# Six split-weight tiles of a two-layer hybrid block: homes of their own at six addresses modulo 128 bytes, instead of three rotating buffers each

## The chip, the cores and the metric

One core of a Trainium2 chip runs the whole program in one launch. The metric is the device time in microseconds of one execution; the median of three runs stands for a kernel.

## The reference, cut to what matters

Two layers, each a mixer and a feed-forward part, on 256 tokens of width 1024, all in float32:

```python
def reference(x, ...):
    for l in range(DEPTH):                       # DEPTH = 2
        h = rms_norm(x, norm_mix_w[l])
        x = x + hybrid_mixer(h, w_in[l], ...)    # attention with a top-64 index, and an SSD scan
        h = rms_norm(x, norm_ffn_w[l])
        x = x + conv_glu_ffn(h, ffn_w_up[l], ...)
    return rms_norm(x, norm_final_w)

def conv_glu_ffn(h, w_up, conv_w, conv_b, w_down):
    u = causal_dwconv(h @ w_up, conv_w, conv_b)
    gate, val = u[..., :FFN_DIM], u[..., FFN_DIM:]
    return (jax.nn.silu(gate) * val) @ w_down
```

Nearly all arithmetic is in products of a 256-token activation with a weight matrix: the wide input projection of the mixer (9,320 columns), three output projections, and the up and down projections of the feed-forward part.

## The kernel before, in words

Activations lie transposed: features on the 128 partitions, the 256 tokens along the free dimension. A float32 product is made of three products in the faster type float32r: both operands are split into a high part (a cast to float32r) and a low part (what the cast left), and high x high, high x low and low x high are summed in PSUM.

The weights come as chunks of at most 128 x 1024 float32, that is 4096 bytes a partition. The list `order` says in which order the chunks are loaded and split. For each chunk, `load_some` issues one DMA into a `raw` buffer (five of them, `RAW_BUFS`), ScalarE casts raw to the high tile `whi` (L199), and VectorE subtracts and writes the low tile `wlo` (L200). `take` does this as far ahead as buffers allow: three pairs (`SPLIT_BUFS`), so the cast for a chunk waits until the products with the chunk three before it are done. Some chunks, those in `early`, are split into activation tiles that happen to be free (names that begin with e: `es`, `ez`, `ex`, `eths`, `ehxh`, `ehxl`, `ebig`, `eXt`, `epT`); they don't use the pairs.

`feed_high` (L370 and L371) multiplies `whi` with the high and the low activation, 16 matmuls a chunk; `feed_low` (L376) multiplies `wlo` with the high activation, 8 a chunk. Here the weight tile is the stationary operand, 128 columns loaded anew for every matmul, and the activation is the moving one, 256 columns. Only in the first five groups of a layer (L549 to L551) is it the other way round: the activation is loaded, and `whi` or `wlo` moves, 308 or 512 columns wide. `n_outer` takes one chunk for one output tile of 128 features, `k_outer` runs four output tiles side by side. Side work (index, attention and scan steps) is put between the products by three lanes of generators, and the order of each engine's instructions is fixed when the program is built.

The moving activations are `hxh`/`hxl` (normed input), `aH`/`aL` (attention out), `bH`/`bL` (SSD out), `mH`/`mL` (merged) and `fH`/`fL` (gated feed-forward), each in tiles of the pool `act`; the tags `s0` to `s3`, `z0` to `z3`, `x0` to `x3` of that pool are reused from stage to stage.

**Addresses.** A pool's tiles stand one behind the other, in the order of their first use, each size rounded up to 32 bytes; so offsets follow from the sizes. Modulo 128 bytes, the raw tiles, all three `whi` and all three `wlo` stand at 64 (the first `whi` at byte 44,608 of a partition). Of the moving tiles, `hxh`, `hxl`, `mH`, `mL`, and all of the tags s, z and x stand at 0, `big0` and `big1` (in which `bL` lies) and the `uh`, `ul` tiles of the first five groups at 64. Below "distance" means how far, modulo 128 bytes, the start of a stationary tile is from that of the moving tile (0 to 64).

Of the kernel before, what the change touches and what calls it, by code (L numbers as in the profile page):

```python
# [10 lines left out]
F32R = mybir.dt.float32r  # L11
# [7 lines left out]
P = 128  # L19
# [14 lines left out]
RAW_BUFS = 5  # L34
SPLIT_BUFS = 3

FIRST_PAIRS = 4


# [23 lines left out]
def hybrid_kernel(ctx: ExitStack, tc: tile.TileContext, a: dict, out: bass.AP):  # L63
# [1 line left out]

    const = ctx.enter_context(tc.tile_pool(name="const", bufs=1))
    wraw = ctx.enter_context(tc.tile_pool(name="wraw", bufs=RAW_BUFS))
    wsp = ctx.enter_context(tc.tile_pool(name="wsp", bufs=SPLIT_BUFS))
    act = ctx.enter_context(tc.tile_pool(name="act", bufs=1))
    tmp = ctx.enter_context(tc.tile_pool(name="tmp", bufs=2))  # L70
    psum = ctx.enter_context(tc.tile_pool(name="psum", bufs=2, space=PSUM))
# [25 lines left out]
    for l in range(L):  # L97
# [11 lines left out]
        for n in range(8):  # L109
            if n == FIRST_PAIRS:  # L110
                for i in range(16):
# [25 lines left out]
        make_early(base, EARLY_MIX)  # L137
        make_early(base + 20, EARLY_CONV)

    st = {"cur": 0, "prep": 0, "dma": 0, "now": 0, "mm": None}  # L140
    lanes = {"norm": [], "attn": [], "scan": []}

    def side(lane, gen, delay):
# [34 lines left out]
    def split_tiles(j):  # L178
        if j in early:
            t0, t1 = early[j]  # L180
            if t0 == t1:
                t = act.tile([P, 2, 8 * 128], F32R, name=f"e{t0}", tag=t0)
                return [t[:, 0], t[:, 1]]
            return [(tmp if t in ("Xt", "pT") else act).tile([P, 8 * 128], F32R, name=f"e{t}", tag=t, bufs=1)
                    for t in (t0, t1)]
        return [wsp.tile([P, 8 * 128], F32R, name=t, tag=t) for t in ("whi", "wlo")]

    def take():
        i = st["cur"]
        with tc.high_priority():  # L190
            load_some()
            while st["prep"] < len(order):
                j = order[st["prep"]]
                if j not in early and sum(k not in early for k in splits) == SPLIT_BUFS:
                    break
                src, b, c = chunks[j]
                hi, lo = (t[:, :b * c] for t in split_tiles(j))
                r = raws.pop(j)
                nc.scalar.copy(out=hi, in_=r)  # L199
                nc.vector.tensor_sub(lo, r, hi.bitcast(F32))  # L200
                splits[j] = [t.rearrange("p (b c) -> p b c", b=b) for t in (hi, lo)]
                st["prep"] += 1
                load_some()
        st["cur"] += 1
        if st["mm"] is not None:
            side_steps()
        return splits.pop(i)
# [197 lines left out]
    for l in range(L):  # L405
# [133 lines left out]
        for c in range(5):  # L539
            n = 308 if c < 2 else 512  # L540
            pss = [pst("acc", [P, n], 4) for _ in range(2)]
            for j in range(4):
                wh, wl = take()
                for kk in range(2):
                    k = 2 * j + kk
                    f, e = k == 0, k == KD - 1
# [5 lines left out]
            for t in range(2):  # L552
                r = nrm.cols[:, t:t + 1]
# [206 lines left out]
        def gate_and_project(n):  # L760
            finish("attn")
            th = gate(tmp.tile([P, T], F32, name="gv", tag="cv", bufs=3))
            ps = n_outer([(lambda k: aH[k // 4][:, k % 4, :], lambda k: aL[k // 4][:, k % 4, :], range(8))])
            nc.vector.scalar_tensor_tensor(mg[n], th, 1.0, ps, op0=OP.add, op1=OP.mult)

        for n in range(FIRST_PAIRS):
            gate_and_project(n)
# [38 lines left out]

        for n in range(FIRST_PAIRS, 8):
            gate_and_project(n)
# [89 lines left out]
    for c in range(2):  # L898
        for h in range(2):
# [4 lines left out]
            r = nrm.cols[:, c:c + 1]  # L904
# [89 lines left out]
```

## Time and profile before

| | us |
|---|---|
| median of 3 runs (lowest to highest) | 1089.46 (1084.34 to 1089.93) |
| profiled execution, its own time | 1091.08 |
| span of that execution | 1089.1 |
| TensorE busy with matmuls (share of the span) | 1064.4 (98%) |
| VectorE busy | 877.9 (81%) |
| ScalarE busy | 696.2 (64%) |
| GpSimd busy | 66.5 (6%) |
| granted TensorE clock, mean | 0.997 |

The span is the time from the first to the last instruction; the profiled execution's own time is 2.0 us longer. A matmul is shown as busy for some 0.28 us, though the next one starts after less than half of that: matmuls overlap, so it is the distance from one start to the next that says how fast they go, and the busy share alone doesn't.

### The profile page before, as it was taken

To read this page: it belongs to the slowest core of one execution; us is meant where nothing else is said; L and a number is where in the kernel's file an instruction comes from. 1 tells how busy PE (TensorE), PEld (TensorE's weight loads), DVE (VectorE), ACT (ScalarE), POOL (GpSimd) and SP (SyncE) were. 2 spreads that over 40 slices of the span, in tenths; PEclk is the share of its full clock that TensorE was granted. 3 is DMA by queue.
4 is the path that set the end of the run, shared out by engine and by line. 5 is a ranking of instruction groups with operands and counts; after the bars stand their busy time and mean duration, and the time that the engine had idled before them with its cause. 6 is when DMAs were issued, how large, how long until landed. Compare 5 with 4: busy or idle time off the path is not lost.

```text
span 1089.1 us, 22471 instructions
## 1 busy us (share of the span) xinstructions
PE 1064.4 (98%) x8704; PEld 1026.2 (94%) x8704; DVE 877.9 (81%) x1755; ACT 696.2 (64%) x1285; POOL 66.5 (6%) x74
## 2 busy tenths in 40 slices
PE   6999999999999999998999999999999999999997
PEld 5789989999999999998997999999999999999997
DVE  6898988879877899885668999887887878888643
ACT  5658878647555576665555699865665556666552
POOL 3000000022000200000100000000310020000010
PEclk9999999999999999999999999999999999999999
DMA  7546444555677346666645654555567761666661
GB/s 266 183 148 213 151 147 156 161 169 175 194 233 251 117 122 195 194 199 211 183 134 176 224 155 139 164 172 155 175 190 216 246 216 45 182 187 191 180 182 48
DMA packets 52841, 191.82 MB, mean 176 GB/s; under 512 B 5952, under 2 KB 6240, under 8 KB 51712
## 3 DMA queue, kind: packets, MB, share of 16 engines
q1 hardware_dynamic: 50832, 180.31, 53.8%
q0 software_dynamic: 1472, 9.17, 2.3%
q8 instruction: 68, 1.11, 0.4%
q10 hardware_dynamic: 432, 0.92, 0.2%
q14 instruction: 37, 0.30, 0.1%
HBM read 189.26 MB, written 1.11 MB: 175 GB/s over the span
## 4 chain that ended last, share of the span: by engine, by line
PE 85%; DMA 5%; ACT 4%; DVE 3%; issue 2%; DVEq 0%; ACTq 0%; POOLq 0%
PE acc L370 23%; PE acc L371 23%; PE acc L376 23%; PE acc L550 3%; PE acc L551 2%; PE acc L549 2%; DMA bc<-prd 2%; DMA raw<-in_wu_dram 2%; PE sb L705 1%; DVE wlo L200 1%; ACT whi L199 1%; PE sa L461 1%; DVE ul L327 1%; PE sa L589 1%; PE sa L614 1%
## 5 line engine op out<-in xcount | busy, mean ns | idle before, releaser
L199 ACT CAST whi<-raw 128x1024 fp32r<-128x1024 f32 (+2 forms) x320 | 331.9, 1040 | 225.1 <-PE acc L371 168.7
L200 DVE TENSOR_TENSOR wlo<-raw,whi 128x1024 fp32r<-128x1024 f32 (+2 forms) x320 | 387.0, 1212 | 107.5 <-ACT whi L199 103.1
L370 PE MATMUL acc<-hxh,whi 128*128 128x256 f32 x1456 | 353.3, 282 | 1.0 <-ACT ths L657 0.9
L371 PE MATMUL acc<-hxl,whi 128*128 128x256 f32 x1456 | 351.2, 281 | 0.0
L370 PEld LDWEIGHTS acc<-hxh,whi 128*128 128x128 f32 x1456 | 274.6, 189 | 2.7 <-issue 1.1
L371 PEld LDWEIGHTS acc<-hxl,whi 128*128 128x128 f32 x1456 | 274.7, 189 | 2.2 <-issue 1.9
L376 PE MATMUL acc<-hxh,wlo 128*128 128x256 f32 x1456 | 202.2, 280 | 0.0
L376 PEld LDWEIGHTS acc<-hxh,wlo 128*128 128x128 f32 x1456 | 183.0, 189 | 0.7 <-issue 0.7
L370 PE MATMUL acc<-fH,whi 128*128 128x256 f32 x352 | 84.6, 280 | 2.8 <-DVE xT L833 2.8
L371 PE MATMUL acc<-fL,whi 128*128 128x256 f32 x352 | 84.4, 280 | 0.0
L649 DVE SCALAR_TENSOR_TENSOR cv<-acc,half,cv 128x255 f32<-128x255 f32 (+2 forms) x144 | 67.1, 474 | 3.9 <-ACT cv L647 3.4
L370 PEld LDWEIGHTS acc<-fH,whi 128*128 128x128 f32 x352 | 66.6, 190 | 3.1 <-issue 3.0
L851 DVE SCALAR_TENSOR_TENSOR cv<-acc,small,cv 128x255 f32<-128x255 f32 (+1 forms) x144 | 68.4, 477 | 1.3
L371 PEld LDWEIGHTS acc<-fL,whi 128*128 128x128 f32 x352 | 66.6, 189 | 0.0
L370 PE MATMUL acc<-bH,whi 128*128 128x256 f32 x256 | 62.4, 280 | 0.1
L371 PE MATMUL acc<-bL,whi 128*128 128x256 f32 x256 | 62.3, 282 | 0.0
L337 POOL TENSOR_TENSOR ssq<-ssq,sq 128x256 f32<-128x256 f32 x30 | 27.1, 904 | 516.8 <-ACT sq L333 516.2
L549 PE MATMUL acc<-whi,uh 128*128 128x512 f32 (+1 forms) x112 | 42.0, 392 | 9.2 <-ACT whi L199 9.2
L376 PE MATMUL acc<-fH,wlo 128*128 128x256 f32 x352 | 50.1, 281 | 0.0
L370 PEld LDWEIGHTS acc<-bH,whi 128*128 128x128 f32 x256 | 48.1, 188 | 0.4 <-issue 0.4
L371 PEld LDWEIGHTS acc<-bL,whi 128*128 128x128 f32 x256 | 48.2, 188 | 0.0
L695 ACT ACTIVATE bc<-bc,nP 128x128 f32<-128x128 f32 x128 | 39.9, 390 | 11.6 <-DMA bc<-prd 11.5
(281 smaller groups left out, 1873.0 us busy)
## 6 DMA issues: line engine op xcount, KB each, us to landing
raw<-in_wu_dram SPq DMA_DIRECT2D x88, 512.0 KB, 3.6
raw<-in_wx_dram SPq DMA_DIRECT2D x48, 512.0 KB, 3.6
raw<-in_wd_dram SPq DMA_DIRECT2D x38, 512.0 KB, 3.7
raw<-in_wz_dram SPq DMA_DIRECT2D x32, 512.0 KB, 3.6
raw<-in_wp_dram SPq DMA_DIRECT2D x32, 512.0 KB, 4.4
raw<-in_wq_dram SPq DMA_DIRECT2D x24, 512.0 KB, 4.5
raw<-in_wgs_dram SPq DMA_DIRECT2D x16, 512.0 KB, 3.6
bc<-prd POOLq DMA_DIRECT2D x8, 1024.0 KB, 7.3
```

The source lines that it names most:

```text
L199: nc.scalar.copy(out=hi, in_=r)
L200: nc.vector.tensor_sub(lo, r, hi.bitcast(F32))
L337: nc.gpsimd.tensor_add(self.acc, self.acc, sq)
L370: nc.tensor.matmul(ps, wh[:, j, :], hi(k), start=first and j == 0, stop=False)
L371: nc.tensor.matmul(ps, wh[:, j, :], lo(k), start=False, stop=False)
L376: st["mm"] = nc.tensor.matmul(ps, wl[:, j, :], hi(k), start=False, stop=last and j == len(ks) - 1)
L549: nc.tensor.matmul(pss[t], nrm.hi(k)[:, s], wh[:, kk, :], start=f, stop=False)
L550: nc.tensor.matmul(pss[t], nrm.hi(k)[:, s], wl[:, kk, :], start=False, stop=False)
L551: st["mm"] = nc.tensor.matmul(pss[t], nrm.lo(k)[:, s], wh[:, kk, :], start=False, stop=e)
L649: nc.vector.scalar_tensor_tensor(v[:, j:], ps[:, :T - j], cw(l, 3 - j, i), v[:, j:], op0=OP.mult, op1=OP.add)
L695: nc.scalar.activation(E[:, h, :], E[:, h, :], AF.Relu, bias=nP[:, c, 8 * g + h:8 * g + h + 1])
L851: nc.vector.scalar_tensor_tensor(v[:, j:], uu[:, :T - j], fw(l, 2 - j, i), v[:, j:], op0=OP.mult, op1=OP.add)
```

## The change

`whi` and `wlo` were one tag each with three rotating buffers. Now there are six tags `w0` to `w5` with one buffer each: chunk after chunk takes the pairs (w0, w1), (w2, w3), (w4, w5) in turn, the first for the high part and the second for the low. Four of the six are 8 elements (32 bytes) larger, and the data begin 4 elements (16 bytes) into those.

```diff
+SHIFTS = ((4, 8), (0, 0), (4, 8), (4, 8), (0, 0), (4, 8))
...
-    wsp = ctx.enter_context(tc.tile_pool(name="wsp", bufs=SPLIT_BUFS))
+    wsp = ctx.enter_context(tc.tile_pool(name="wsp", bufs=1))
...
-    st = {"cur": 0, "prep": 0, "dma": 0, "now": 0, "mm": None}
+    st = {"cur": 0, "prep": 0, "dma": 0, "now": 0, "mm": None, "home": 0}
...
-        return [wsp.tile([P, 8 * 128], F32R, name=t, tag=t) for t in ("whi", "wlo")]
+        r = st["home"]
+        st["home"] = (r + 1) % SPLIT_BUFS
+        ts = []
+        for i in (2 * r, 2 * r + 1):
+            first, pad = SHIFTS[i]
+            t = wsp.tile([P, 8 * 128 + pad], F32R, name=f"w{i}", tag=f"w{i}")
+            ts.append(t[:, first:first + 8 * 128])
+        return ts
```

Worked out from the sizes, with the pool still at byte 44,608, the data of w0 to w5 begin at 80, 96, 112, 16, 32 and 48 modulo 128. The pool grows by 4 x 32 = 128 bytes, so every tile behind it moves up by 128 bytes and keeps its place modulo 128.

## Rows read from the trace of the kernel before

**Rows 1.** The page: busy time of each engine, its share of the span, instructions

```profile
PE 1064.4 (98%) x8704; PEld 1026.2 (94%) x8704; DVE 877.9 (81%) x1755; ACT 696.2 (64%) x1285; POOL 66.5 (6%) x74
```

**Rows 2.** The page: the chain that ended last, its shares by engine

```profile
PE 85%; DMA 5%; ACT 4%; DVE 3%; issue 2%; DVEq 0%; ACTq 0%; POOLq 0%
```

**Rows 3.** Stretches: from:to us, length, PE busy (matmuls), clock, DMA share, GB/s

```profile
81.70:89.60 7.90, 7.90 (x72) 1.00 0.96 321
388.60:482.20 93.60, 93.60 (x828) 1.00 0.63 188
916.20:1016.40 100.20, 100.20 (x854) 1.00 0.60 179
```

**Rows 4.** Timeline of PE, FFN of first layer: start us, us busy, line, tiles

```profile
450.36 1.07 PE L376 MATMUL acc<-hxh,wlo 128*128 128x256 f32 x8
...
453.08 0.96 PE L376 MATMUL acc<-hxh,wlo 128*128 128x256 f32 x7
```

**Rows 5.** Timeline of PE, FFN of second layer

```profile
1000.37 0.28 PE L370 MATMUL acc<-hxh,whi 128*128 128x256 f32 x1
...
1003.19 0.28 PE L370 MATMUL acc<-hxh,whi 128*128 128x256 f32 x1
```

**Rows 6.** Timeline of PE, a chunk split into activation tiles x0, x1

```profile
89.76 0.28 PE L370 MATMUL acc<-hxh,ex 128*128 128x256 f32 x1
...
91.68 1.12 PE L376 MATMUL acc<-hxh,ex 128*128 128x256 f32 x8
```

**Rows 7.** Timeline of PE, down projection of first layer, chunks of one output tile

```profile
526.42 0.28 PE L370 MATMUL acc<-fH,whi 128*128 128x256 f32 x1
...
528.31 1.10 PE L376 MATMUL acc<-fH,wlo 128*128 128x256 f32 x8
529.25 0.28 PE L370 MATMUL acc<-fH,whi 128*128 128x256 f32 x1
...
531.98 0.28 PE L370 MATMUL acc<-fH,whi 128*128 128x256 f32 x1
```

**Rows 8.** Timeline of PE, SSD output projection

```profile
317.56 1.11 PE L376 MATMUL acc<-bH,wlo 128*128 128x256 f32 x8
...
320.40 0.40 PE L376 MATMUL acc<-bH,wlo 128*128 128x256 f32 x2
```

**Rows 9.** Timeline of PE, transposes (128 columns of float32)

```profile
683.25 1.04 PE L607 MATMUL sa<-ident,lg 128*128 128x128 f32 x8
684.12 0.28 PE L714 MATMUL sb<-Cm,Bm 128*128 128x128 f32 x1
```

**Rows 10.** Timeline of PE, 308-column matmuls with an early tile moving

```profile
556.86 0.30 PE L549 MATMUL acc<-ehxh,uh 128*128 128x308 f32 x1
...
557.71 0.31 PE L549 MATMUL acc<-ehxh,uh 128*128 128x308 f32 x1
...
558.56 0.31 PE L549 MATMUL acc<-ehxl,uh 128*128 128x308 f32 x1
```

**Rows 11.** Timeline of PE, 512-column matmuls with the split weights moving

```profile
567.30 0.39 PE L549 MATMUL acc<-whi,uh 128*128 128x512 f32 x1
...
568.66 0.39 PE L549 MATMUL acc<-whi,uh 128*128 128x512 f32 x1
```

**Rows 12.** Groups by line: busy us, mean ns of one, idle before

```profile
L370 PE MATMUL acc<-hxh,whi 128*128 128x256 f32 x1456 | 353.3, 282 | 1.0 <-ACT ths L657 0.9
...
L370 PE MATMUL acc<-fH,whi 128*128 128x256 f32 x352 | 84.6, 280 | 2.8 <-DVE xT L833 2.8
...
L370 PE MATMUL acc<-bH,whi 128*128 128x256 f32 x256 | 62.4, 280 | 0.1
```

**Rows 13.** Line L199, the casts: ns min/median/max, first and last start

```profile
L199 ACT CAST whi<-raw x320: 687/1052/1069, 8.5 to 1070.7; 128x1024 fp32r<-128x1024 f32 x154, 128x768 fp32r<-128x768 f32 x4, 128x616 fp32r<-128x616 f32 x2
...
L199 ACT CAST ez<-raw x4: 1048/1048/1053, 302.0 to 841.3; 128x1024 fp32r<-128x1024 f32 x4
```

**Rows 14.** Waits: who for whom, us in total, times, longest

```profile
ACT whi L199 <- PE acc L371: 168.7, 143, 5.4
```

## The prediction, made before the change was run

> **What bounds the kernel now.** Read the page's busy times first: TensorE is busy with matmuls for 98% of the span, and weight loads fill 94% beside it [rows 1]. The chain that ended last is 85% TensorE [rows 2]: the other engines and the DMAs matter only where they stop it. Since matmuls overlap in the profile, the next view is the timeline of PE, and there the distance between starts. The reader is to see that matmuls of one shape, 128 columns loaded and 256 moved, run at three different steady speeds:
>
> - 24 of them (one chunk) in 453.08 - 450.36 = 2.72 us, 113.3 ns each [rows 4];
> - 24 in 2.82 us, 117.5 ns each, in the same stage of the second layer [rows 5];
> - 16 in 1.92 us, 120.0 ns each, with an early tile as the weights [rows 6].
>
> The stretches confirm it over hundreds of matmuls. A matmul shows as busy for 0.28 us, so some 2.4 of each count had begun earlier: 93.60 / 825.6 = 113.4 ns and 100.20 / 851.6 = 117.7 ns, at a granted clock of 1.00 in both [rows 3]. So neither the clock nor the work differs. Two levels stand at distance 64 (all `whi` and `wlo` against `hxh` and `hxl`), 120.0 at distance 0 (`x0`, `x1` against `hxh`, `hxl`). At distance 64 a level, once entered, stays: 94 us on one, 100 us on the other. In the down projection of the first layer it changes with the moving tile: 24 in 2.83 us (117.9 ns) for the chunk that meets `fH0` and `fH1`, then 24 in 2.73 us (113.8 ns) for the next [rows 7]. With `bH` at distance 64 and `bL` at distance 0 in turn a chunk takes 2.84 us, 118.3 ns each [rows 8]. What makes the levels, the trace doesn't show.
>
> **The change part by part.**
>
> *Six homes for three rotating buffers.* Removed and added instructions: none. A pair is used again three chunks later, as before. The cast that waits for TensorE to leave its pair, 143 times and 168.7 us in all [rows 14], goes on waiting for the same chunk. On ScalarE the work for the next chunks is queued behind that wait, as now; it is covered by three chunks of matmuls, 8.2 us at [rows 4]. I take nothing; if reuse lost one chunk of lead the cover would still be 5.4 us against a cast of 1.05 us [rows 13] and the subtraction behind it.
>
> *Casts and subtractions at other addresses.* The cast takes 1052 ns (median) into `whi` at 64 and 1048 ns into `ez` at 0 [rows 13]. Other offsets I take at the same. Even 50 ns more on each would be hidden: ScalarE is busy 64% and VectorE 81% of the span [rows 1].
>
> *The products with `whi` and `wlo` as weights.* This is the whole of the change in time. Their number: 3 x (1456 + 352 + 256) = 6,192 with `hx`, `f` and `b` moving [rows 12] (one of three lines with like counts stands for each), and by the code 3 x (128 + 128) = 768 with `a` and `m`, so 6,960. One ns on each is 6.96 us. Their mean now, an estimate from the stretches: on the fast level some 860 of the up projection of the first layer, half of the 1,056 of the down projections, and about half of the 2,260 (by the code) in the mixer's stages with many short stops (a fast piece of them is the first stretch of [rows 3], 7.90 / 69.6 = 113.5 ns), together some 2,500; the other 4,460 on the slow level. (2,500 x 113.3 + 4,460 x 117.8) / 6,960 = 116.2 ns.
>
> After the change the weights stand at 80, 96, 112, 16, 32 and 48, the moving tiles at 0 (`bL` at 64). Distances to 0: 48 and 32 for the first pair, 16 and 16 for the second, 32 and 48 for the third. No row has 256-column matmuls at these. Bounds from the nearest rows: 108.8 ns below (eight transposes with 128 columns loaded each, 0.87 us [rows 9], the fastest full-width matmuls of the trace) and 120.0 above [rows 6]. So the term lies between (108.8 - 116.2) x 6.96 = -51 us and +26 us. The row nearest to the new offsets has another shape, 308 columns with an early tile moving. Its first six matmuls have the activation at 64 and the moving data at 0, distance 64; the next six start 1,232 bytes later, at 80, distance 16. Both take 0.85 us, 141.7 ns each [rows 10]. By that row distance 16 costs and gains nothing.
>
> What does change for certain is that the distance is no longer the same from one tile to the next: it moves twice a chunk. So I expect a level not to stay for 94 or 100 us, but to be drawn anew at each tile. With the two levels seen at distances other than 0 drawn evenly: (113.3 + 117.8) / 2 = 115.6 ns, 0.6 ns below now, -4 us.
>
> *The 308- and 512-column products.* The 512-column ones take 1.36 / 6 = 226.7 ns [rows 11], all at distance 0 now; there are 288 by the code. If leaving distance 0 gave each the 6.7 ns between [rows 6] and [rows 4], -1.9 us; the other sign is as large. I take 0. The 308-column ones with split weights are 48; nothing.
>
> *Sum.* -4 us on the profiled execution's 1091.08 is 1087; that execution was 1.6 us above the median, so 1085.5 in its terms; I write 1086. A lottery of levels also fits the spread of the runs: one up projection on the other level is 860 x 4.5 ns = 3.9 us, of the 5.6 between the lowest and the highest run.
>
> A page of the Trainium skill, "TensorE: Matmul & The Clock Gate" (Part 2, Step-by-step), says that weight loads and the moving operand have separate read ports of SBUF and that a load takes no bandwidth from the running matmul. By it addresses would not matter and the change would be worth nothing: the time stays at 1089.5. [Rows 4] and [rows 6], same shape, 113.3 and 120.0 ns, don't agree with so plain a picture.
>
> **The rivals.**
>
> *Nearer is worse.* Distance 64, where all split weights stand now, gives 116.2 ns in the mean, distance 0 gives 120.0. If the cost rises evenly as the tiles come nearer, the new distances, 32 in the mean, give 118.1 ns: +1.9 x 6.96 = +13 us, 1103; all on the level of [rows 6], 1116. It decides wherever the tile nearest to the moving one (w2 and w3, distance 16) runs at 119 ns or more. For it: the only row at distance 0 is the slowest. Against it: [rows 10], and that [rows 8], with half of its `whi` products at distance 0, is only 0.5 ns above the slow level.
>
> *The fast level everywhere.* If the slow level needs equal distances to hold itself, it dies out: (113.3 - 116.2) x 6.96 = -20 us, 1069. For it: the fast level held for 94 us. Against it: the slow one is entered again and again at the tiles `fH0` and `fH1`.
>
> *No collision left.* If all three levels are one kind of collision that starts at multiples of 64 bytes provoke, 16-byte offsets could free the matmuls to the 108.8 ns of [rows 9]: -51 us, 1038. Against it: [rows 10] at distance 16 is as slow as at 64. The same page of the skill (Back-to-back issue gap) gives N / 2.4 + 2.5 ns for a warm matmul alone, 109.2 ns for 256 columns; [rows 9] come to that, no 256-column row does.
>
> *It does nothing.* The levels have a cause that these addresses don't touch: 1089.5, give or take the 4 us of the lottery.
>
> **How the numbers follow.** The measurement can tell about 0.5%, 5.5 us, from no change. Levels drawn anew: 0.37, at 1086, its own range 1078 to 1096 (115.0 to 117.1 ns); that splits into 0.11 faster, 0.20 same, 0.06 slower. Nearer is worse: 0.30, of which 0.01 same. Fast level everywhere: 0.22. No collision left: 0.08. Nothing: 0.03. Faster 0.41, same 0.24, slower 0.35. The range 1065 to 1112 leaves out the case without collisions and the far end of the slower one, together under 0.2.
>
> **What would show it.** In the up projection of both layers the distance between starts, tile by tile: mixed levels within one chunk and like totals for the two layers speak for my forecast; 119 to 120 ns at w2 and w3 and less at w0 and w5 for nearness; 113.3 throughout or 109 for the faster rivals; one level held over 90 us again for no effect. If the waits of ScalarE for TensorE are fewer or longer than in [rows 14] by more than the matmuls explain, the homes did change the order, and the first step was wrong. The prediction fails as a whole if the mean over the 6,960 products is below 113 or above 119.5 ns.

## The result, and the profile after

| | median (lowest to highest), us | runs |
|---|---|---|
| before | 1087.0 (1084.34 to 1089.93) | 4 |
| after | 1099.84 (1097.35 to 1102.34) | 4 |

The ratio after / before is 1.0118, 95% interval 1.0076 to 1.0159: slower, by 12.8 us between the medians. The forecast was 1086, 3.5 us below the 1089.46 that stood for the kernel before when it was made.

The line numbers of the changed kernel are 9 higher: L199 and L200 are L208 and L209, and L370, L371, L376 are L379, L380, L385. First the busy times and the chain of the profiled execution (1099.86 us), which answer to [rows 1, 2]:

```profile
PE 1076.2 (98%) x8704; PEld 1037.5 (94%) x8704; DVE 878.8 (80%) x1755; ACT 697.3 (64%) x1285; POOL 66.7 (6%) x74
...
PE 89%; DMA 4%; DVE 3%; ACT 2%; issue 1%; DVEq 0%; ACTq 0%; POOLq 0%
```

As many instructions as before, VectorE and ScalarE as busy as before, and TensorE 11.8 us longer on the same 8,704 matmuls. So the time went into the matmuls themselves. One line of the casts and one of the waits answer to [rows 13, 14]:

```profile
L208 ACT CAST w<-raw x320: 687/1048/1069, 8.5 to 1079.3; 128x1024 fp32r<-128x1024 f32 x154, 128x768 fp32r<-128x768 f32 x4, 128x616 fp32r<-128x616 f32 x2
...
ACT w L208 <- PE acc L380: 169.7, 141, 5.5
```

The time for which one matmul is shown as busy says nothing here, since matmuls overlap. What counts is how many start in a stretch. The stretches of the up projection, as in [rows 3] (length, matmul time and count, clock):

```profile
388.60:482.20 93.60, 93.60 (x799) 93.60 (x798) 82.34 (x140) 63.26 (x105) 0.00 (x0) 1.00 0.59 179
...
919.30:1012.90 93.60, 93.60 (x797) 93.60 (x796) 83.01 (x146) 63.16 (x108) 0.00 (x0) 1.00 0.56 169
```

With the same reckoning as for [rows 3], 93.60 / 796.6 = 117.5 ns in the first layer and 93.60 / 794.6 = 117.8 in the second: the first layer has lost its fast stretch (x828 before), the second is where it was, both at full clock. The starts on PE in the second layer, one row for each split tile in turn, w0 to w5 and w0 again, answer to [rows 5]:

```profile
999.47 0.28 PE L379 MATMUL acc<-hxh,w 128*128 128x256 f32 x1
...
1001.33 1.10 PE L385 MATMUL acc<-hxh,w 128*128 128x256 f32 x8
1002.27 0.28 PE L379 MATMUL acc<-hxh,w 128*128 128x256 f32 x1
...
1004.18 1.11 PE L385 MATMUL acc<-hxh,w 128*128 128x256 f32 x8
1005.13 0.28 PE L379 MATMUL acc<-hxh,w 128*128 128x256 f32 x1
...
1007.02 1.10 PE L385 MATMUL acc<-hxh,w 128*128 128x256 f32 x8
1007.96 0.28 PE L379 MATMUL acc<-hxh,w 128*128 128x256 f32 x1
```

w0 takes 1.86 / 16 = 116.3 ns, w2 1.91 / 16 = 119.4, w4 1.89 / 16 = 118.1; all 72 together 8.49 / 72 = 117.9. In the first layer the tiles rank otherwise. The 16 matmuls with w2 there, up to the first one with w3, answer to [rows 4]:

```profile
451.39 0.28 PE L379 MATMUL acc<-hxh,w 128*128 128x256 f32 x1
...
453.27 0.40 PE L385 MATMUL acc<-hxh,w 128*128 128x256 f32 x2
```

Here w2 takes 1.88 / 16 = 117.5 ns, 2 ns less than in the second layer, and so it does in the first layer's other chunks. The speed differs from tile to tile, but no tile runs at 113.3. Last the 512-column matmuls, answering to [rows 11]:

```profile
568.86 0.40 PE L558 MATMUL acc<-w,uh 128*128 128x512 f32 x1
...
570.25 0.40 PE L558 MATMUL acc<-w,uh 128*128 128x512 f32 x1
```

1.39 / 6 = 231.7 ns, where 226.7 stood.

Adding up every distance from one start to the next in the two traces (the order of the matmuls is the same in both) gives the whole difference between the two profiled executions, us:

| | before | after | difference |
|---|---|---|---|
| 6,960 products, while running (under 131 ns) | 793.5 | 805.5 | +12.0 |
| stops within them | 33.1 | 31.1 | -2.0 |
| 288 512-column matmuls, while running | 59.7 | 60.5 | +0.8 |
| other matmuls and stops | 185.8 | 183.7 | -2.1 |

The mean over the 6,960 products went from 116.24 to 117.95 ns. The executions are 8.8 us apart, the medians 12.8, because the profiled execution of before, 1091.08, was 4 us above its median.

### The profile page after: what moved, and what is told of

It is laid out like the page before. It is cut to its first block, busy times and chain, and to the rows that moved or that the text cites. A ratio compares the mean times of both kernels' runs of the same rounds, so it can differ in the third digit from the quotient of the medians.

```text
span 1097.9 us, 22471 instructions
## 1 busy us (share of the span) xinstructions
PE 1076.2 (98%) x8704; PEld 1037.5 (94%) x8704; DVE 878.8 (80%) x1755; ACT 697.3 (64%) x1285; POOL 66.7 (6%) x74
## 4 chain that ended last, share of the span: by engine, by line
PE 89%; DMA 4%; DVE 3%; ACT 2%; issue 1%; DVEq 0%; ACTq 0%; POOLq 0%
PE acc L379 25%; PE acc L380 24%; PE acc L385 24%; PE acc L559 3%; PE acc L558 2%; PE acc L560 2%; DMA raw<-in_wu_dram 2%; PE sb L714 2%; DVE w L209 1%; PE sa L598 1%; PE sa L623 1%; DMA raw<-in_wi_dram 1%; PE sa L470 1%; ACT w L208 1%; DVE ul L336 1%
## 5 line engine op out<-in xcount | busy, mean ns | idle before, releaser
L208 ACT CAST w<-raw 128x1024 fp32r<-128x1024 f32 (+2 forms) x320 | 331.1, 1037 | 236.1 <-PE acc L380 169.7
L209 DVE TENSOR_TENSOR w<-raw,w 128x1024 fp32r<-128x1024 f32 (+2 forms) x320 | 387.2, 1213 | 111.8 <-ACT w L208 105.8
L379 PE MATMUL acc<-hxh,w 128*128 128x256 f32 x1456 | 357.8, 282 | 0.0
L380 PE MATMUL acc<-hxl,w 128*128 128x256 f32 x1456 | 356.1, 282 | 0.0
L380 PEld LDWEIGHTS acc<-hxl,w 128*128 128x128 f32 x1456 | 273.7, 188 | 2.2 <-issue 1.9
L379 PEld LDWEIGHTS acc<-hxh,w 128*128 128x128 f32 x1456 | 273.7, 188 | 1.5 <-issue 0.8
L385 PE MATMUL acc<-hxh,w 128*128 128x256 f32 x1456 | 204.6, 281 | 0.0
L385 PEld LDWEIGHTS acc<-hxh,w 128*128 128x128 f32 x1456 | 185.3, 188 | 0.7 <-issue 0.7
L379 PE MATMUL acc<-fH,w 128*128 128x256 f32 x352 | 86.4, 282 | 1.9 <-DVE xT L842 1.9
L380 PE MATMUL acc<-fL,w 128*128 128x256 f32 x352 | 86.4, 283 | 0.0
L379 PEld LDWEIGHTS acc<-fH,w 128*128 128x128 f32 x352 | 66.7, 190 | 2.1 <-issue 2.1
L380 PEld LDWEIGHTS acc<-fL,w 128*128 128x128 f32 x352 | 66.6, 190 | 0.0
L379 PE MATMUL acc<-bH,w 128*128 128x256 f32 x256 | 62.2, 281 | 0.3 <-ACT w L208 0.2
L380 PE MATMUL acc<-bL,w 128*128 128x256 f32 x256 | 62.2, 282 | 0.0
L385 PE MATMUL acc<-fH,w 128*128 128x256 f32 x352 | 51.0, 284 | 0.0
L379 PEld LDWEIGHTS acc<-bH,w 128*128 128x128 f32 x256 | 48.4, 189 | 0.7 <-ACT w L208 0.3
L380 PEld LDWEIGHTS acc<-bL,w 128*128 128x128 f32 x256 | 48.1, 188 | 0.0
```

The source lines that it names most:

```text
L379: nc.tensor.matmul(ps, wh[:, j, :], hi(k), start=first and j == 0, stop=False)
L380: nc.tensor.matmul(ps, wh[:, j, :], lo(k), start=False, stop=False)
L385: st["mm"] = nc.tensor.matmul(ps, wl[:, j, :], hi(k), start=False, stop=last and j == len(ks) - 1)
```

## The experiments

From here on **place** is the start of a split weight tile less the start of the moving tile, modulo 256 bytes. Modulo 256 the split weights of before stand at 64, and of the moving tiles `hx`, the x and z tags at 0 (place 64), the s tags at 128 (place 192), `bL` at place 0. The change grows the pool by 128 bytes, so it does two things: it gives six offsets, and it moves everything behind by 128 bytes, which modulo 128 is nothing and modulo 256 is half the way round. The four corners of these two, each with its ratio to before:

| | pool not grown (modulo 256) | grown by 128 |
|---|---|---|
| all weights at 64 | before; with homes 0.9993 (0.9966 to 1.002) | 1.0069 (1.0034 to 1.0104) |
| six offsets | 1.0159 (1.0119 to 1.02) | the change, 1.0118 (1.0076 to 1.0159) |

**The growth alone.** Six homes, no offsets, 128 bytes at the end of the pool:

```diff
-SHIFTS = ((4, 8), (0, 0), (4, 8), (4, 8), (0, 0), (4, 8))
+SHIFTS = ((0, 0), (0, 0), (0, 0), (0, 0), (0, 0), (0, 32))
```

> The six homes and the 128 bytes by which the pool grows are kept, the offsets are undone: all six tiles begin at 64 modulo 128, as before the change. Theory A (the offsets are what costs): as before the change, 1087 us within 5, levels of 113.3 and 117.8 ns held over whole stretches. Theory B (the homes or the shift of every later tile by 128 bytes costs, since the addresses matter modulo 256 or more): about 1100 us, as with the change.

1096.55 us (1094.64 to 1097.42) against 1087.83. All distances modulo 128 were those of before, and yet most of the loss was there. Both up projections sit on the slow level, 93.60 / 794.6 = 117.8 ns:

```profile
388.60:482.20 93.60, 93.60 (x797) 93.60 (x796) 82.37 (x140) 63.36 (x105) 0.00 (x0) 1.00 0.59 179
...
919.30:1012.90 93.60, 93.60 (x797) 93.60 (x796) 82.27 (x141) 62.87 (x104) 0.00 (x0) 1.00 0.58 176
```

So the distance modulo 128, on which the whole prediction was built, is the wrong measure, provided that the six homes cost nothing by themselves; the next run shows that.

**The homes alone.**

```diff
+SHIFTS = ((0, 0),) * 6
```

> The six homes alone: all tiles at 64 modulo 128, and the pool doesn't grow, so that every later tile stands where it stood before the change. Theory A (addresses modulo 256 of weights and moving tile, taken relative to each other, set the speed): 1087 us within 5, as before the change. Theory B (six homes in place of three buffers cost by themselves): 1096, as with all six at 64 and the pool 128 bytes longer.

1085.72 us (1082.8 to 1093.0), the same as before within 0.35%. In this profile both up projections are fast, 93.60 / 826.6 = 113.2 ns:

```profile
388.60:482.20 93.60, 93.60 (x829) 93.60 (x828) 85.62 (x145) 65.21 (x109) 0.00 (x0) 1.00 0.61 185
...
919.30:1012.90 93.60, 93.60 (x828) 93.60 (x827) 85.38 (x144) 63.84 (x105) 0.00 (x0) 1.00 0.64 192
```

**A sweep of places.** The kernel before, with 256 spare bytes in each buffer; in the up projection the place changes every four chunks (96 matmuls with `hx` moving):

```diff
+PLAN = [[(p, p) for p in ps for _ in range(4)]
+        for ps in ((64, 80, 96, 112, 128, 144, 160, 176, 64), (64, 192, 208, 224, 240, 0, 16, 32, 48))]
...
```

> As before the change, but in the up projection whi and wlo of four chunks running begin at one place, and the next four at another: 64, 80, 96, 112, 128, 144, 160, 176, 64 modulo 256 in the first layer, 64, 192, 208, 224, 240, 0, 16, 32, 48 in the second; the moving tiles stand at 0. Theory A1 (nearer is worse): within a run of four chunks the distance between starts is steady, 113.3 or 117.8 ns at 64 and 192, rising evenly to 120.0 at 128 and 0, 118 to 119 at distance 16 and 32. Theory A2 (changing from tile to tile is what costs): 113.3 or 117.8 ns in every run of four chunks, with dearer matmuls only in the first few after each change. Theory A3 (multiples of 64 bytes are the bad ones): below 113.3 ns at 16, 32 and 48 beside a multiple of 64.

The one execution took 1092.61 us; the reading is in the starts. A row stands for the first matmul at each place, 64, 80, 96, 112 and 128 in the first layer, and 192, 208, 224, 240, 0, 16 and 32 in the second:

```profile
386.71 0.29 PE L379 MATMUL acc<-hxh,whi 128*128 128x256 f32 x1
...
397.61 0.28 PE L379 MATMUL acc<-hxh,whi 128*128 128x256 f32 x1
...
409.01 0.28 PE L379 MATMUL acc<-hxh,whi 128*128 128x256 f32 x1
...
420.40 0.28 PE L379 MATMUL acc<-hxh,whi 128*128 128x256 f32 x1
...
431.92 0.28 PE L379 MATMUL acc<-hxh,whi 128*128 128x256 f32 x1
...
929.34 0.28 PE L379 MATMUL acc<-hxh,whi 128*128 128x256 f32 x1
...
940.22 0.28 PE L379 MATMUL acc<-hxh,whi 128*128 128x256 f32 x1
...
951.42 0.28 PE L379 MATMUL acc<-hxh,whi 128*128 128x256 f32 x1
...
962.62 0.28 PE L379 MATMUL acc<-hxh,whi 128*128 128x256 f32 x1
...
974.14 0.28 PE L379 MATMUL acc<-hxh,whi 128*128 128x256 f32 x1
...
985.65 0.28 PE L379 MATMUL acc<-hxh,whi 128*128 128x256 f32 x1
...
997.01 0.28 PE L379 MATMUL acc<-hxh,whi 128*128 128x256 f32 x1
```

Each difference is divided by 96. Place 64: 10.90 / 96 = 113.5 ns. Place 80: 11.40 / 96 = 118.8. Place 112: 11.52 / 96 = 120.0. Place 192: 10.88 / 96 = 113.3. Places 208 and 224: 11.20 / 96 = 116.7. Place 240: 120.0. Place 16: 11.36 / 96 = 118.3. The table adds the other places, by the last 48 matmuls of each stretch, and those of the two runs below that try more of them:

| place | ns | place | ns |
|---|---|---|---|
| 0 | 120.0 | 128 | 118.7 |
| 16, 32 | 118.3 | 144 | 118.3 |
| 48 | 117.8 to 118.3 | 160 | 120.0 |
| 56, 60 | 117.8, 119.6 | 176 | 118.1 |
| **64** | **113.3 or 117.8** | 184, 188 | 117.8, 118.3 |
| 68, 72 | 118.3 | **192** | **113.3 or 117.8** |
| 80, 96 | 118.8, 118.6 | 196, 200 | 117.8, 120.0 |
| 112 | 120.0 | 208, 224 | 116.7 |
| | | 240 | 120.0 |

Places 0 (six stretches), 16 (three), 80, 176 and 208 (two each) came out the same every time; 48 held 117.8 twice and 118.3 twice, 64 and 192 held either of two levels, and every other place was tried once. The level of 113.3 was seen at 64 and at 192 only, and no split weight of the change stands there. The levels hold for stretches of one place. Where tiles take turns they are less exact: w2 of the change stands at 240, where the table has 120.0, and took 119.4 ns in the second layer and 117.5 in the first. Weighting this table with the number of products that the change puts at each place (1,328 at 208, 752 at 224, 1,280 at 240, 1,264 at 32, and so on) gives 118.2 ns; measured are 117.95. That the difference of the two addresses counts, and not that of the weights alone, is borne out by the means over all products, 118.2 reckoned and 117.95 measured: the sweep moved the weights under a fixed `hx`, the change moved both.

**Offsets with the growth made up to 256.** 128 bytes more, so that the tiles behind keep their place modulo 256 (room from two small tiles sharing a buffer):

```diff
-SHIFTS = ((4, 8), (0, 0), (4, 8), (4, 8), (0, 0), (4, 8))
+SHIFTS = ((4, 8), (0, 0), (4, 8), (4, 8), (0, 0), (4, 40))
...
```

> The change, with another 128 bytes behind the last tile, so that every later tile moves by 256 bytes and keeps its place modulo 256; for room, one small tile shares a buffer with another that is used in another stage. Theory A (relative place modulo 256): the weights now stand 80, 96, 112, 144, 160 and 176 above most moving tiles; by the runs of four chunks at these places 118.8, 118.7, 119.9, 118.3, 119.9 and 118.1 ns, in the mean 119.1 or 3 ns over before, so 1107 us. Theory C (distance modulo 128 alone): as the change, 1100. Theory D (the 128 bytes by which the later tiles move are what costs, the offsets nothing): 1087.

1105.53 us (1104.6 to 1106.79) against 1087.09, as the theory of places modulo 256 had it (1107), and slower than the change itself: with the six offsets the 128 bytes of growth cost nothing, they win back a part of the loss. The moving tile `hx` now meets the weights at 80, 96, 112, 144, 160 and 176. The table's levels with this kernel's counts give 119.0 ns, measured are 118.96; in the up projection 93.60 / 784.6 = 119.3 and 93.60 / 786.6 = 119.0:

```profile
388.60:482.20 93.60, 93.60 (x787) 93.60 (x787) 81.25 (x140) 62.55 (x103) 0.00 (x0) 1.00 0.57 172
...
919.30:1012.90 93.60, 93.60 (x789) 93.60 (x788) 82.59 (x151) 62.48 (x105) 0.00 (x0) 1.00 0.53 158
```

**What is run before the fast places.** The sweep's kernel with another plan:

```diff
+        for ps in ((0, 64, 0, 192, 0, 64, 0, 192, 0), (16, 64, 16, 192, 48, 64, 48, 192, 64))]
...
```

> As the sweep, with other places: 0, 64, 0, 192, 0, 64, 0, 192, 0 in the first layer and 16, 64, 16, 192, 48, 64, 48, 192, 64 in the second, four chunks each. Theory A1 (64 and 192 each have both levels, and which one comes is decided at the entry, alike each time for like entries): 120.0 at 0, 118.3 at 16, 117.8 at 48, and at 64 and 192 either 113.3 or 117.8, the same on each return from the same place. Theory A2 (192 is fast as such, 64 a lottery): 113.3 at every run of 192.

1095.22 us, one execution. The first matmul at 0, 64, 0, 192 and 0 of the first layer:

```profile
387.33 0.28 PE L379 MATMUL acc<-hxh,whi 128*128 128x256 f32 x1
...
398.84 0.28 PE L379 MATMUL acc<-hxh,whi 128*128 128x256 f32 x1
...
410.15 0.28 PE L379 MATMUL acc<-hxh,whi 128*128 128x256 f32 x1
...
421.67 0.28 PE L379 MATMUL acc<-hxh,whi 128*128 128x256 f32 x1
...
432.55 0.28 PE L379 MATMUL acc<-hxh,whi 128*128 128x256 f32 x1
```

From 0, place 64 comes out slow, 11.31 / 96 = 117.8, and place 192 fast, 10.88 / 96 = 113.3; so both times that each was tried. In the second layer, once each, both were slow from 16, both came out fast from 48, and a fast stretch stayed fast from 192 to 64. Which of the two levels is taken at 64 or 192 is thus settled at the entry, and in this execution it went with the place that ran before, on one or two tries each. That place isn't all that counts: in the kernel before, the up projections of both layers are entered at 64 from the same kind of chunk, and one came out fast and the other slow.

**Places close to 64 and 192.**

```diff
+        for ps in ((64, 60, 56, 48, 64, 68, 72, 80, 64), (192, 188, 184, 176, 192, 196, 200, 208, 192))]
...
```

> As the sweep, with places near 64 and 192: 64, 60, 56, 48, 64, 68, 72, 80, 64 in the first layer and 192, 188, 184, 176, 192, 196, 200, 208, 192 in the second. Theory A (the fast level needs exactly half of the 128 bytes): 113.3 or 117.8 only at 64 and 192, 116 to 119 at all others. Theory E (a level between, or faster, at places that are no multiple of 16): some place under 113.3 ns, or a level that holds at 4 or 8 bytes beside 64.

1094.63 us, one execution. First matmuls at 64, 60, 56 and, in the second layer, at 192 and 196:

```profile
385.18 0.28 PE L379 MATMUL acc<-hxh,whi 128*128 128x256 f32 x1
...
396.07 0.29 PE L379 MATMUL acc<-hxh,whi 128*128 128x256 f32 x1
...
407.55 0.28 PE L379 MATMUL acc<-hxh,whi 128*128 128x256 f32 x1
...
964.01 0.28 PE L379 MATMUL acc<-hxh,whi 128*128 128x256 f32 x1
...
974.90 0.28 PE L379 MATMUL acc<-hxh,whi 128*128 128x256 f32 x1
```

64: 10.89 / 96 = 113.4; 60: 11.48 / 96 = 119.6; 192: 10.89 / 96 = 113.4; 196, in the table, 117.8. Four bytes off, and the fast level is gone. (The other two stretches at 192, the first of the layer and the one after 208, were slow, 117.8.) No place ran below 113.3.

**All products at one place.** The kernel before with gaps, so that every moving tile has the split weights at place 64 (before: 896 of the 6,960 at 192 and 256 at 0), and a second one with all at 192, in which gap0 has 16 elements for 48:

```diff
+        if not l:
+            act.tile([P, 48], F32, name="gap0", tag="gap0")
         tok = [act.tile([P, 8 * T], F32, name=f"big{t}", tag=f"big{t}")[:, :1856] for t in range(2)]
...
+            act.tile([P, 48], F32, name="gap1", tag="gap1")
...
+            act.tile([P, 32], F32, name="gap2", tag="gap2")
...
```

> The kernel before (three rotating buffers at 64) with gaps of 192, 192 and 128 bytes in front of big0/big1, of the s tags and of hx, x, z (room from letting kd share the tag bt), so that every moving 256-column tile stands 64 bytes below the split weights modulo 256: all 6,960 products at place 64, none at 192 (896 before) or 0 (256 before). Theory A (place modulo 256 sets the level, 113.3 or 117.8 at 64 and at 192; which of the two is settled by what ran before): the 256 products at 0 lose 120.0 - 117.8 or more, the 896 at 192 may come to the fast level; gain 0.6 us at least if the share of the fast level stays as it was, up to 1152 x 4.5 ns = 5 us if all of these become fast; and the up projection may fall on either level, 3.9 us a layer. So 1078 to 1091, about 1084. Theory B (only the distance modulo 128 matters, as the prediction had it): only bL changes, -0.6 us, 1087.

1084.47 us (1081.79 to 1089.85), ratio 0.9974 (0.9952 to 0.9997): a small gain, of the expected size.

> As the kernel with everything at place 64, with a gap of 64 bytes instead of 192 in front of big0/big1 and the same gaps behind, arranged so that every moving 256-column tile stands at 128 modulo 256 and the split weights at 64: all 6,960 products at place 192. Theory A as it stands (two levels at 192 as at 64, settled by what ran before): if the history is like that of the run with the 128-byte growth alone, where 92% of the products at 192 were on the slow level, 6,960 x (117.5 - 116.2) = +9 us, 1096; if 192 is entered from the early tiles as it was entered from place 0 in the run on entries (fast both times), mostly fast, 1070 to 1080. Theory B (distance modulo 128 only): no difference from the one at place 64.

1087.38 us (1081.81 to 1093.93), ratio 1.0003 (0.9977 to 1.0028): between the two forms of the theory, and not the 1096 of the run with the growth alone. Against the kernel before, a place of 192 is therefore no slower by itself; the 2.9 us between the medians of the two runs here lie within their overlapping ranges. The SSD output projection and both up projections of the one at 64, and then the SSD output projection of the one at 192:

```profile
299.00:335.00 36.00, 35.83 (x305) 35.65 (x304) 28.14 (x42) 19.82 (x25) 0.00 (x0) 1.00 0.76 246
388.60:482.20 93.60, 93.60 (x829) 93.60 (x828) 85.69 (x144) 65.21 (x108) 0.00 (x0) 1.00 0.62 187
...
919.30:1012.90 93.60, 93.60 (x828) 93.60 (x827) 85.42 (x146) 64.35 (x107) 0.00 (x0) 1.00 0.61 186
```

```profile
299.00:335.00 36.00, 36.00 (x313) 35.92 (x313) 28.86 (x43) 20.36 (x27) 0.00 (x0) 1.00 0.75 244
```

In the same stretch of the mixer 313 matmuls start at place 192 and 305 at 64, while the up projections are alike (828 or 829 in each).

**The better place for each stage.** Place 192 for the last four pairs of the attention, the SSD output projection and the output projection, 64 for the rest:

```diff
-            first, pad = SHIFTS[i]
-            t = wsp.tile([P, 8 * 128 + pad], F32R, name=f"w{i}", tag=f"w{i}")
+            first = 32 * ((i + (j in far)) % 2)
+            t = wsp.tile([P, 8 * 128 + 32], F32R, name=f"w{i}", tag=f"w{i}")
...
```

> The kernel with everything at place 64, with six homes (shown to cost nothing) each 128 bytes larger, so that a chunk may stand at place 64 or 192: the last eight gate and projection chunks of the attention, the SSD output projection (b moving) and the output projection (m moving) stand at 192, the rest at 64. Theory A (the level at 64 and at 192 is settled by what ran before, and after the stop near 281 us it is the slow one at 64 and the fast one at 192, as the profiles of the two runs before show, in both layers): against the run with everything at 64, 2 x 86 products of hx and a at 113.3 for 117.8 (0.8 us), 2 x 384 of b at 115.3 for 117.7 (1.8 us), 2 x 192 of m at 113.3 for about 116.7 (1.3 us), together 3.9 us: about 1080.5, ratio to the kernel before about 0.993. Theory L (the levels at 64 and 192 are a free lottery at each stop, and the two profiles differed by chance): 1084.5 as with everything at 64.

1087.26 us (1081.15 to 1093.96), ratio 0.9978 (0.995 to 1.0005): the gain of 3.9 us did not show. Where the expectation had most to say, in the mixer of the first layer, it came true (x312 for x305), but the up projection of the second layer fell to the slow level in this execution (x797; 829 start in the same stretch of the first layer):

```profile
299.00:335.00 36.00, 35.94 (x312) 35.76 (x311) 28.65 (x43) 20.30 (x26) 0.00 (x0) 1.00 0.75 246
...
517.00:522.50 5.50, 5.29 (x25) 5.32 (x26) 4.47 (x9) 3.99 (x9) 1.62 (x2) 0.50 0.80 270
...
919.30:1012.90 93.60, 93.60 (x797) 93.60 (x796) 81.99 (x139) 62.85 (x104) 0.00 (x0) 1.00 0.61 182
```

The twelve times stand in three clusters, 5 from 1081.2 to 1084.0, 4 from 1087.2 to 1090.5 and 3 from 1092.3 to 1094.0. One layer's up and down projections are 1,392 products, and 1,392 x 4.44 ns = 6.2 us, about the step between the clusters; that the level of each layer's entry differs from execution to execution would make them. No run shows that, since a trace was kept of one execution of each kernel. Nor can it be all: the execution shown (1092.3) has one layer fast and yet lies in the slowest cluster. The third row, in the down projection of the first layer, shows another cost: after TensorE had stood idle for 4.0 us the granted clock is at its lower level, 1.2 GHz, and 25 matmuls start in 5.5 us, 51 in the kernel with everything at 192, where the clock stayed at 1.00. 26 fewer at 5.5 / 51 = 0.108 us each are 2.8 us. It doesn't tell the slowest cluster from the others, though: in the same stretch the clock is 0.69 with 32 matmuls in the kernel before and 0.69 with 22 in the one with everything at 64.

**Place 0 ahead of the fast place.** By the run on entries, place 0 and then 192 gives the fast level. Seven chunks a layer stand at 0 (the first, 11th and 16th of z, the second of the SSD output projection, the first of the output projection, the first of the up projection with `hx`, the first of the second part of the down projection), the rest from z on at 192:

```diff
+        place.update((j, 192) for j in range(start, len(chunks)))
+        place.update((start + j, 0) for j in (0, 10, 15, 25, 40, 56, 103))
...
+            first = (place.get(j, 64) - 64 - 192 * i) % 256 // 4
+            t = wsp.tile([P, 8 * 128 + (80 if i == 5 else 48)], F32R, name=f"w{i}", tag=f"w{i}")
...
```

> The kernel with everything at place 64, with six larger homes, so that a chunk may stand at place 64, 192 or 0. From the start of the z projection to the end of a layer the split weights stand at 192, and seven chunks a layer stand at 0: the first, 11th and 16th of z, the second of the SSD output projection, the first of the output projection, the first of the up projection that has hx moving, and the first of the second part of the down projection. Theory A (what ran before settles the level, and place 0 before place 192 gives the fast one, as in the run on entries both times): the up and down projections are fast in every run, so the three clusters of the run with places by stage (about 1082, 1087.5 and 1093) become one; against its lowest cluster, z gains 2 x 294 x 4.4 ns = 2.6 us, b and m in the mean about 1.5 us, and the chunks at 0 cost 14 x 24 x 6.7 ns = 2.2 us: about 1080, all runs below 1085, ratio about 0.992. Theory L (the level is drawn anew in each execution whatever ran before): three clusters again, median about 1087.

1081.24 us (1076.28 to 1084.91), ratio 0.9941 (0.9921 to 0.9961): faster than both kernels, all twelve times below 1085, with no cluster at 1087 or 1092. That the chunks at 0 did it isn't shown by itself: no run left them out and kept the rest. Both up projections are fast; the SSD output projection came out slow in both layers of this profile (x300), though its second chunk was at 0:

```profile
299.00:335.00 36.00, 35.36 (x300) 35.19 (x300) 27.37 (x40) 19.16 (x25) 0.00 (x0) 1.00 0.75 242
388.60:482.20 93.60, 93.60 (x828) 93.60 (x827) 85.68 (x144) 64.28 (x107) 0.00 (x0) 1.00 0.64 193
...
919.30:1012.90 93.60, 93.60 (x828) 93.60 (x827) 84.87 (x144) 64.29 (x106) 0.00 (x0) 1.00 0.65 193
```

Four output tiles run side by side there, so that the chunk at 0 is mixed with matmuls of a chunk at 192. But a chunk at 0 isn't needed to make the stage slow. In the run with everything at 192, which has no chunk at 0, the 24 matmuls of the chunk before this stage take (291.78 - 289.06) / 24 = 113.3 ns:

```profile
289.06 0.28 PE L370 MATMUL acc<-aH,whi 128*128 128x256 f32 x1
...
291.78 0.28 PE L370 MATMUL acc<-bH,whi 128*128 128x256 f32 x1
```

```profile
297.00:313.00 16.00, 16.00 (x138) 16.00 (x138) 11.86 (x17) 9.78 (x13) 0.00 (x0) 1.00 0.69 215
...
317.00:337.00 20.00, 20.00 (x179) 20.00 (x178) 17.07 (x27) 13.21 (x18) 0.00 (x0) 1.00 0.77 254
```

At 294.95 and 296.36 us two products of the norm (`sb<-dg,ones`) come in among the matmuls of the stage, and behind them these run at 16.00 / 135.6 = 118.0 ns. Near 314.5 us one distance between starts is 0.2 us, and then they are fast again, 20.00 / 176.6 = 113.3. In the run entered from 0 they are slow behind the two products as well, but a stop of 0.9 us from start to start there doesn't bring the fast level back, 20.00 / 169.6 = 117.9:

```profile
317.00:337.00 20.00, 20.00 (x172) 20.00 (x171) 16.40 (x25) 12.95 (x18) 0.00 (x0) 1.00 0.77 247
```

The level turns to slow at these two products in both layers of the run with everything at 192, and in both of the run with places by stage: the place that ran before is not all that settles it. What the products do to it is not known.

## Why the prediction was wrong

**The homes cost nothing: right.** Homes alone 0.9993; the wait of the cast 169.7 us in 141 times against 168.7 in 143.

**The casts cost nothing: right.** 1048 ns median against 1052, and VectorE's busy time is 0.9 us longer in all.

**The mean before, 116.2 ns: right.** 116.24 by the starts.

**The step that failed: "I expect a level not to stay for 94 or 100 us, but to be drawn anew at each tile", with the two levels "drawn evenly", 115.6 ns.** Two speeds at place 64 had been taken for a property of the matmuls wherever the weights stand. They belong to place 64 and its twin 192. At every other place tried the levels lie between 116.7 and 120.0, and the fast one is not among them. So there was nothing to draw from: the change did not mix the fast level in; it shut it out. The term was +1.71 ns and +12.0 us for the -0.6 ns and -4 us of the forecast. An estimate of the loss from the means by stage: some 2,400 of the 6,960 products of the kernel before ran on the fast level, and 2,400 x 4.5 ns are 10.8 of the 12.0 us. The bounds, 108.8 and 120.0, held.

**What the step rested on.** [Rows 10] were read as "distance 16 costs and gains nothing". They are matmuls of another shape with stationary and moving data the other way round, and for the second of their two places (112 modulo 256) no 256-column row existed; the level of one shape did not carry to the other. The one row of the right shape away from 64 was [rows 6], 120.0 ns, and it was the better guide: away from 64 things are slower. [Rows 7] held a sign that 128 is not the period: by the rule that gives the addresses, `fH0` and `fH1` put the weights at place 192 and the next chunk's tiles at 64, one distance modulo 128, and the two chunks ran at 117.9 and 113.8 ns.

**What was left out: the 128 bytes.** The prediction took a move by 128 bytes as no move, because modulo 128 nothing changes. By itself it costs 0.69%. It shifts `hx`, x and z from place 64 to 192; the fast level exists there too, but the entries to the up projections came out slow in the execution profiled. It is not a term to be added to that of the offsets: with them, the grown pool is the faster one, 1.0118 against 1.0159. The 512-column matmuls were forecast as 0, within 1.9, and took +0.8 us. Either half of the change is enough for that: means over running ones are 228.7 ns with the homes alone, 232.4 with the growth alone, 231.9 with the offsets and 256 bytes.

**The rivals.** "Nearer is worse" had the time nearly right (1103, 118.1 ns) for a reason that falls: places 240 and 16 are equally near and run at 120.0 and 118.3, and 32 is no better than 16. Its sign, w2 above 119 ns, is there in the second layer of the trace after and not in the first, 117.5. That a lottery of levels fits the spread of the runs still stands, but as a fit: no trace of two executions of one kernel was kept. In the range that the prediction gave for levels drawn anew, 1078 to 1096 with 115.0 to 117.1 ns, the lower end is a slip: 115.0 ns gives (115.0 - 116.2) x 6.96 = -8 us, or 1081. A page of the Trainium skill, "TensorE: Matmul & The Clock Gate" (Part 2, Step-by-step), says that a weight load takes no read bandwidth from the running matmul; what the prediction drew from it, that addresses would then not matter, does not agree with the runs: the same matmuls take 113.3 to 120.0 ns by their start addresses.

**What stays open.** Why 64 and 192 have a fast level, what physical part the two streams share, and what in an entry settles the level: place 0 before 192 gave the fast one in all four up-projection entries of the two traces that have it, but the place that ran before does not decide alone. Of the run with the growth alone it is not known why both up projections were slow when those of the kernel with everything at 192 were not.

## What to carry to other kernels

Where TensorE is the bound and small matmuls run at two speeds at one clock, measure the distance between starts for each relative address of weights and moving data, on the very shape, before moving any tile; here one stage of one kernel was enough for the table. An edit to a buffer's size also moves all that is allocated behind it, so an experiment on addresses has to hold those fixed, and "the same modulo 128" was not the same. A fast level that was found by luck is easily lost by an edit that moves its addresses. One kernel here, with both the places and what runs ahead of them chosen, had all its times below 1085 us; which of the two did it, and whether it carries over, is not shown.

## What was not expected of the hardware

- Start addresses matter to 4 bytes (place 64: 113.4 ns, place 60: 119.6) and over a period of at least 256 bytes.
- Two speeds at one place, each held over 800 matmuls and settled at the entry, at a granted clock of 1.00. By 117.8 less 113.3 ns, an estimate for the 1,392 products of one layer's feed-forward part is 6.2 us from one level to the other.
- Two matmuls of another kind among hundreds can end the fast level: 113.3 ns before them and 117.8 behind them, at the same places and the same clock.
